# One decoder step on one core: v and a of an RWKV-7 chunk transposed together from a side-by-side copy, and the two rank-64 products written in turns

## Chip, core and metric

One core of a Trainium2 chip runs the whole step. The metric is the device time of one execution in microseconds (us); less is better. TensorE is called PE, its weight loads PEld, VectorE DVE, ScalarE ACT, GpSimd POOL; SP is the SyncE queue that issues most DMAs.

## What is computed

The step is one layer over 1024 prompt tokens and 8 sequences of 8 sample tokens (1088 columns): an input projection into four token mixers (HGRN2, RWKV-7, a convolution module, RG-LRU), gates, output projection and an MLP, all in float32. The change touches the RWKV-7 mixer (8 heads of 64) and one scratch tile of the residual update. Cut from the reference:

```python
r, k, v, wd, ad, gd = split(rwm)                     # 512, 512, 512, 64, 64, 128 columns
log_w = -RW_DECAY_SCALE * sigmoid(rw_w0 + tanh(wd) @ rw_w_up)     # decay, rank 64
a = sigmoid(rw_a0 + ad @ rw_a_up)                                  # rate, rank 64
...
def step(s, inp):                                    # per token; s is [value, key] of a head
    rt, wt, kt, vt, kkt, at = inp
    sa = einsum("bhvk,bhk->bhv", s, -kkt)
    s = s * wt[:, :, None, :] + sa[..., None] * (kkt * at)[:, :, None, :] + vt[..., None] * kt[:, :, None, :]
    return s, einsum("bhvk,bhk->bhv", s, rt)
```

## The kernel before

Activations lie with channels on the 128 partitions and tokens along the row. Large products run as float32 split into two fp32r halves (tiles `pg`, weights `whi` and `wlo`, made from a staged load `wst` by ACT and DVE; `wst` has three buffers, `whi` and `wlo` four). Small products (`sm`, `tr`, `G`, `p1`, `wt`, `pu` and so on) are plain float32, for which the hardware makes two passes over PE; a transpose by `nc.tensor.transpose` takes one.

The mixers are Python generators. `ROUNDS` says in which order their pieces are written; a scheduler that simulates a timeline then interleaves the instructions of all of them on each engine, and the order on every engine is fixed from then on. PE so works on chunk products of the projections and gates (`pg`) while the chains of the mixers run on the other engines.

`rw_block(j)` handles two heads, 128 partitions, and runs four times (j = 0 to 3). In order:

- Two rank-64 products, decay and rate. `up[:, 0, :]` holds the decay matrix on partitions 0 to 63 and the rate matrix on 64 to 127, `wd` the two inputs in the same way. `small_mm` runs the rate product over three token tiles (364, 362 and 362 columns), each copied out of PSUM by ACT with a sigmoid, and then the decay product. PSUM tiles of the pool `pm` (tag `m`) have three buffers.
- From these, scaled forms per chunk of 64 tokens: `ar[chunk]` with the columns a (index 0, minus kk times decay; this is the "a" of the change, not the rate) and r (index 1), and `kb` with k and b. Products `G` per chunk and head, each on 64 of the 128 rows, alternate the heads, four chunks (8 products) to a group with two PSUM tiles. A triangular inverse follows: `za`, `At`, 31 steps on DVE with the scratch `tm`, then `zx`, `X1`, and the products `zq` and `zz`.
- A loop over 17 chunks, first number 16 (the sample tokens), then 0 to 15. On every even chunk it handles two chunks at once: v and a are transposed into one PSUM tile `tr` so that v's tokens lie on partitions 0 to 63 and a's on 64 to 127, kb is transposed beside them, and ACT copies the result to `vk` (two buffers). The products `p1` and `wt` use it, two chunks at a time. Per chunk then `pu`, a copy by ACT into `vk` (`vk<-pu`), `pst`, the state `St` by DVE, and `pyr`; `pu` of the next chunk needs `St`. So 32 pairs of chunks and 4 single chunks are transposed in the four blocks.

`add_resid` adds a scaled PSUM tile to the residual; its scratch `t64` is written and read by DVE.

Of the kernel before, what the change touches and what calls it, by code (L numbers as in the profile page):

```python
# [9 lines left out]
F32 = mybir.dt.float32  # L10
# [3 lines left out]
AF = mybir.ActivationFunctionType  # L14
# [10 lines left out]
CHUNKS = ((0, 364), (364, 362), (726, 362))  # L25
# [57 lines left out]
def c3(a):  # L83
    return a.rearrange("p (c t) -> p c t", t=64)


def s3(a):
    return a.rearrange("p (s t) -> p s t", t=8)


class Net:
# [382 lines left out]
    def rw_block(self, j):  # L474
        nc = self.nc
        J = slice(j * 128, j * 128 + 128)
        blk = self.c("blk")
        up = self.rp.tile([128, 2, 128], F32, name="up", bufs=1)
# [9 lines left out]
        def parts(x):  # L488
# [6 lines left out]
        ar = pair("ar", 8)  # L495
        ch = lambda x, c: x[c // 8][:, c % 8]

        a, sg, wd = self.flat("a", 4), self.flat("sg", 5), self.flat("wd", 2)
        nc.sync.dma_start(wd[:, :NT], self.wdd)
        kk, inv = self.flat("kk", 6), self.flat("inv", 3)  # L500
        self.act(kk[:, :NT], kF[:, :NT], AF.Square, scale=self.p("rw_k_k", j))
        self.small_mm(up[64:128, 0, :], wd[64:128, :],
                      lambda ps, n0, n: self.act(a[:, n0:n0 + n], ps[:, :n], AF.Sigmoid, bias=self.p("rw_a0", j)))
        self.small_mm(up[0:64, 0, :], wd[0:64, :],
                      lambda ps, n0, n: self.act(sg[:, n0:n0 + n], ps[:, :n], AF.Sigmoid, bias=self.p("rw_w0", j)))
        self.log_table()

        self.small_mm(blk, kk, lambda ps, n0, n: nc.vector.tensor_scalar(
# [43 lines left out]
        for c in range(0, 17, 4):  # L552
            w = min(4, 17 - c)
            pss = [self.pmt("G") for _ in range(2)]
            for cc in range(w):
                for h in range(2):
                    H = slice(64 * h, 64 * h + 64)
                    o = cc * 128
# [13 lines left out]
        v = self.flat("v", 12)  # L572
# [10 lines left out]
        nc.sync.dma_start(At, za.rearrange("a u i t -> (a u) i t"))  # L583
        nc.gpsimd.memset(Zu_t[0:68, 0:1024], 0.0)
        nc.gpsimd.memset(Zu_t[0:68, 0:1024:33], 1.0)
        tm_t = self.rp.tile([128, 256], F32, name="tm")
        for i in range(31):
            r, m = i + 1, 31 - i
            tm = tm_t[0:68, 0:r * m].rearrange("p (r m) -> p r m", m=m)
# [11 lines left out]
        for g in range(5):  # L601
            u0, w = 8 * g, (8 if g < 4 else 2)
# [3 lines left out]
        for u0 in range(0, 34, 16):  # L606
            w = min(16, 34 - u0)
            ps = self.pmt("zq")
# [16 lines left out]
        ident = self.c("ident")  # L625
# [3 lines left out]
        for c in [16] + list(range(16)):  # L629
            G = Gc(c)  # L630
            if c % 2 == 0:
                w = min(2, 17 - c)
                vk2 = self.rp.tile([128, 2, 2, 128], F32, name="vk", bufs=2)
                ps = self.pmt("tr")
                for cc in range(w):
                    o = cc * 256
                    nc.tensor.transpose(ps[0:64, o:o + 128], v[:, (c + cc) * 64:(c + cc) * 64 + 64], ident)
                    self.mm(ps[64:128, o:o + 128], ch(ar, c + cc)[:, 0, :], ident)
                    nc.tensor.transpose(ps[:, o + 128:o + 256], ch(kb, c + cc).rearrange("p a t -> p (a t)"), ident)
                self.act(vk2[:, 0:w].rearrange("p c a t -> p (c a t)"), ps[:, :w * 256])  # L640
                p12 = self.rp.tile([128, 2, 128], F32, name="p12", bufs=2)
                wt2 = self.wz[(c // 2) % 2]
                ps, ps2 = self.pmt("p1"), self.pmt("wt")
                for cc in range(w):
                    for h, Hc in enumerate(Hs):
                        self.mm(ps[64:128, cc * 128 + 64 * h:cc * 128 + 64 * h + 64], Gc(c + cc)[0:64, h, 0:64],
                                vk2[0:64, cc, 0, Hc])
                        self.mm(ps2[Hc, cc * 64:cc * 64 + 64], vk2[64:128, cc, 0, Hc], Zc(c + cc, h))
                self.act(p12[64:128, 0:w].rearrange("p c t -> p (c t)"), ps[64:128, :w * 128])
                for h, Hc in enumerate(Hs):  # L650
                    self.act(wt2[Hc, 0:w, h, :], c3(ps2[Hc, 0:w * 64]))
            cc = c % 2
            VA, KBT = vk2[:, cc, 0, :], vk2[:, cc, 1, :]

            if c < 16:
                pu = self.pc.tile([128, 512], F32, name="pu", tag="pc")
                for h, Hc in enumerate(Hs):
                    self.mm(pu[64:128, Hc], Zc(c, h), p12[64:128, cc, Hc], start=h == 0, stop=c == 0)
                if c:
                    for h, Hc in enumerate(Hs):  # L660
                        self.mm(pu[64:128, Hc], wt2[:, cc, h, :], St, start=False, stop=True)
            else:
                pu, px = self.pmt("pus"), self.pmt("px")
                for q in range(8):
                    for h, Hc in enumerate(Hs):
                        self.mm(px[Hc, 8 * q:8 * q + 8], ss[Hc, q, :], wt2[Hc, cc, h, 8 * q:8 * q + 8])
                ut = self.rp.tile([128, 64], F32, name="ut")
                self.act(ut, px[:, :64])
                self.mm(pu[64:128, 0:128], ut, ident, start=True, stop=False)
                for h, Hc in enumerate(Hs):  # L670
                    self.mm(pu[64:128, Hc], Zc(c, h), p12[64:128, cc, Hc], start=False, stop=True)
            self.act(VA[64:128, :], pu[64:128, 0:128])

            So = St
            if c < 16:
                pst = self.pc.tile([128, 512], F32, name="pst", tag="pc")
                for Hc in Hs:
                    self.mm(pst[Hc, 0:64], KBT[:, Hc], VA[:, Hc])
                Sn = self.rp.tile([128, 64], F32, name="St", bufs=3)
                if c == 0:  # L680
                    nc.vector.tensor_scalar(Sn, pst[:, 0:64], dec[:, 0:1], None, op0=OP.mult)
                else:
                    sp = self.rp.tile([128, 64], F32, name="sp", bufs=2)
                    nc.gpsimd.tensor_scalar(sp, St, dec[:, c:c + 1], None, op0=OP.mult)
                    self.stt(Sn, pst[:, 0:64], dec[:, c:c + 1], sp, OP.mult, OP.add)
                St = Sn
                if c == 15:
                    nc.gpsimd.dma_start(self.A["o_rw"][j, :, 0, :], St)

            if c % 8 == 0:  # L690
                py = self.py.tile([128, 512], F32, name="pyr", tag="py")
            yc = slice((c % 8) * 64, (c % 8) * 64 + 64)
            for h, Hc in enumerate(Hs):
                self.mm(py[Hc, yc], VA[:, Hc], G[:, h, 64:128], start=c % 8 == 0, stop=False)
            if c == 16:
                for q in range(8):
                    for Hc in Hs:
                        self.mm(py[Hc, 8 * q:8 * q + 8], ss[Hc, q, :], ar[2][Hc, 0, 1, 8 * q:8 * q + 8],
                                start=False, stop=q == 7)
            elif c:  # L700
                for Hc in Hs:
                    self.mm(py[Hc, yc], So[Hc, :], ch(ar, c)[Hc, 1, :], start=False, stop=True)
            if c % 8 == 7:
                self.act(y[:, (c - 7) * 64:(c + 1) * 64], py)
            elif c == 16:
                self.act(y[:, T:NT], py[:, :64])
                vx_t = self.flat("vx", 1)
                pst = self.pmt("pss")
                for h, Hc in enumerate(Hs):
                    vx = vx_t[:, h * 512:h * 512 + 512].rearrange("p (q v) -> p q v", v=64)  # L710
                    self.tt(vx, VA[:, Hc].unsqueeze(1).to_broadcast([128, 8, 64]),
                            self.c("bm").unsqueeze(2).to_broadcast([128, 8, 64]), OP.mult)
                    self.mm(pst[Hc, :], KBT[:, Hc], vx_t[:, h * 512:h * 512 + 512])
                self.tt(ss, ss, pst.rearrange("p (q v) -> p q v", v=64), OP.add)
                self.tt(ss, ss, dec[:, 16:24].unsqueeze(2).to_broadcast([128, 8, 64]), OP.mult)
                nc.gpsimd.dma_start(self.A["o_rw"][j, :, 1:9, :], ss)
# [370 lines left out]
def trunk_kernel(ctx: ExitStack, tc: tile.TileContext, A):  # L1087
# [158 lines left out]
    def add_resid(r, n0, ps, n, mt, gi, fresh=False):  # L1246

        e = min(n, T - n0)
        rp, pp = (r, ps) if e == n else (r[:, :e], ps[:, :e])
        if fresh:  # L1250
            net.act(rp, pp, scale=net.modp(gi, mt))
        else:
            net.stt(rp, pp, net.modp(gi, mt), rp, OP.mult, OP.add)
        if e < n:
            t = s3(r[:, e:n]) if fresh else net.kp.tile([128, 8, 8], F32, name="t64", tag="t64", bufs=2)
            net.tt(t, ps[:, e:n].rearrange("p (s t) -> p s t", t=8), net.mods(gi, mt), OP.mult)
            if not fresh:
                net.tt(r[:, e:n], r[:, e:n], t.rearrange("p s t -> p (s t)"), OP.add)
# [288 lines left out]
```

## Time and profile before

| | |
|---|---|
| Median of 3 runs | 2547.24 us (2545.0 to 2548.16) |
| The profiled execution, its own time | 2543.26 us |
| Its span, first to last instruction | 2541.4 us |
| Mean granted TensorE clock | 0.986 of full speed |
| PE busy | 2454.6 us, 97% |
| DVE, ACT, POOL busy | 54%, 41%, 13% |

The profile shows one execution. Times in its rows are us from the span's start unless they say ns. A timeline row has start, length, engine, line, operation, tile written and tiles read, size and count; rows of one kind that follow each other are merged, so that a length is that of the group. PE's lengths overlap, because products are pipelined and their ends are modelled: what a product costs is read from its start to the start of what follows it. [...] In a row of waits the engine and tile before the arrow wait for what stands behind it.

### The profile page before, as it was taken

The numbers are of one execution on the slowest core, as the hardware profiler recorded it, in microseconds if no ns is written. First come the engines' busy times: TensorE is split into PE (matmuls) and PEld (weight loads), VectorE is DVE, ScalarE is ACT, GpSimd is POOL, SyncE is SP. The second block draws the span as 40 slices with busy tenths as digits, with TensorE's granted clock in tenths as the row PEclk, the third lists the DMA queues.
The fourth block names the chain that finished last, engine by engine and source line by source line (L and its number), as shares of the span: only waits on it lengthen the run. The fifth ranks groups of instructions, "written<-read, shape, count | busy, mean of one in ns | idle before, by whom it ended". The sixth has DMA issues, their size and how long they took to land.

```text
span 2541.4 us, 46737 instructions
## 1 busy us (share of the span) xinstructions
PE 2454.6 (97%) x19222; PEld 2259.4 (89%) x19222; DVE 1381.6 (54%) x2536; ACT 1038.2 (41%) x1855; POOL 320.4 (13%) x503
## 2 busy tenths in 40 slices
PE   6999999999999999999999999999999999999996
PEld 2897889897898988989887999998899999999996
DVE  6664626647355645266552757668755552422246
ACT  4512434422454224453234753336666664111114
POOL 3101110102100011101021100000222221000003
PEclk9999999999999999999999999999999999999998
DMA  6322132122221222212312555533556657434144
GB/s 241 119 81 80 50 107 68 61 69 80 100 68 65 73 82 66 95 62 77 92 48 71 186 168 187 205 112 103 156 154 162 157 152 256 136 135 186 62 158 129
DMA packets 166550, 296.01 MB, mean 116 GB/s; under 512 B 38824, under 2 KB 78712, under 8 KB 166336
## 3 DMA queue, kind: packets, MB, share of 16 engines
q1 hardware_dynamic: 115920, 213.33, 26.0%
q0 software_dynamic: 47104, 74.44, 9.6%
q10 hardware_dynamic: 3312, 5.25, 0.6%
q8 instruction: 151, 2.47, 0.4%
q14 instruction: 63, 0.52, 0.1%
HBM read 211.29 MB, written 81.66 MB: 115 GB/s over the span
## 4 chain that ended last, share of the span: by engine, by line
PE 82%; DVE 9%; DMA 4%; ACT 2%; issue 2%; SPq 0%; DVEq 0%; ACTq 0%
PE pg L107 54%; PE pa L107 5%; PE pe L107 4%; PE sm L107 3%; DVE X L101 2%; PE ada L107 2%; PE pc L107 2%; PE pu L107 2%; PE pb L107 2%; DMA zx<-At 1%; DVE wlo L101 1%; PE pyr L107 1%; PE G L107 1%; PE tr L107 1%; PE po L107 1%
## 5 line engine op out<-in xcount | busy, mean ns | idle before, releaser
L107 PE MATMUL pg<-Hh,whi 128*128 128x362 f32 (+1 forms) x1872 | 627.7, 335 | 4.7 <-ACT Hh L98 4.2
L107 PE MATMUL pg<-Hh,wlo 128*128 128x362 f32 (+1 forms) x1872 | 631.3, 337 | 0.0
L107 PE MATMUL pg<-Hl,whi 128*128 128x362 f32 (+1 forms) x1872 | 623.3, 336 | 0.7 <-DVE Hl L104 0.6
L98 ACT ACTIVATE whi<-wst 128x512 fp32r<-128x512 f32 (+1 forms) x404 | 249.8, 619 | 620.9 <-PE pg L107 546.5
L101 DVE TENSOR_TENSOR wlo<-wst,whi 128x512 fp32r<-128x512 f32 (+1 forms) x404 | 279.8, 694 | 389.1 <-ACT whi L98 384.6
L107 PEld LDWEIGHTS pg<-Hh,whi 128*128 128x128 f32 x1872 | 356.2, 190 | 15.4 <-ACT Hh L98 6.2
L107 PEld LDWEIGHTS pg<-Hh,wlo 128*128 128x128 f32 x1872 | 356.6, 190 | 13.8 <-issue 6.5
L107 PEld LDWEIGHTS pg<-Hl,whi 128*128 128x128 f32 x1872 | 355.3, 190 | 10.8 <-issue 2.5
L107 PE MATMUL pg<-ah,whi 128*128 128x272 f32 x960 | 276.3, 290 | 4.0 <-ACT whi L98 4.0
L107 PE MATMUL pg<-ah,wlo 128*128 128x272 f32 x960 | 277.2, 290 | 0.9 <-DVE wlo L101 0.9
L107 PE MATMUL pg<-al,whi 128*128 128x272 f32 x960 | 273.9, 290 | 0.0
L107 PEld LDWEIGHTS pg<-ah,whi 128*128 128x128 f32 x960 | 181.9, 190 | 4.9 <-ACT whi L98 4.7
L107 PEld LDWEIGHTS pg<-ah,wlo 128*128 128x128 f32 x960 | 182.1, 190 | 1.7 <-DVE wlo L101 1.5
L107 PEld LDWEIGHTS pg<-al,whi 128*128 128x128 f32 x960 | 180.4, 190 | 0.0
L104 DVE SCALAR_TENSOR_TENSOR cacc<-u,pv,cacc 128x1024 f32<-128x1024 f32 x120 | 154.3, 1286 | 2.1
L104 DVE SCALAR_TENSOR_TENSOR R<-pg,mod,R 128x544 f32<-128x544 f32 (+2 forms) x120 | 65.7, 570 | 134.7 <-PE pg L107 134.6
L107 PE MATMUL pg<-yh,whi 128*128 128x362 f32 (+1 forms) x384 | 127.6, 332 | 0.9 <-DVE gt L101 0.9
L107 PE MATMUL pg<-yh,wlo 128*128 128x362 f32 (+1 forms) x384 | 126.6, 330 | 0.0
L107 PE MATMUL pg<-yl,whi 128*128 128x362 f32 (+1 forms) x384 | 126.2, 329 | 0.0
L1172 POOL DMA_DIRECT2D g<-gst x96 | 53.5, 558 | 400.5 <-ACT gst L98 396.8
L98 ACT ACTIVATE gst<-pg 128x362 f32<-128x362 f32 (+1 forms) x96 | 45.5, 474 | 132.4 <-PE pg L107 112.3
L104 DVE SCALAR_TENSOR_TENSOR St<-pst,dec,sp 128x64 f32<-128x64 f32 x60 | 17.0, 283 | 136.4 <-PE pst L107 135.3
(450 smaller groups left out, 4884.0 us busy)
## 6 DMA issues: line engine op xcount, KB each, us to landing
wst<-w SPq DMA_DIRECT2D x136, 256.0 KB, 2.9
wst<-w_in SPq DMA_DIRECT2D x92, 256.0 KB, 3.0
gt<-g SPq DMA_DIRECT2D x32, 544.0 KB, 3.8
wst<-w_gate SPq DMA_DIRECT2D x64, 256.0 KB, 3.5
adaw<-ada SPq DMA_DIRECT2D x32, 512.0 KB, 3.9
ah<-ah POOLq DMA_DIRECT2D x60, 272.0 KB, 2.8
al<-al POOLq DMA_DIRECT2D x60, 272.0 KB, 4.3
ah<-ah SPq DMA_DIRECT2D x30, 544.0 KB, 9.7
```

The lines of the kernel that those rows point to most:

```text
L98: return self.nc.scalar.activation(out, in_, func, bias=bias, scale=scale)
L101: return self.nc.vector.tensor_tensor(out, a, b, op=op)
L104: return self.nc.vector.scalar_tensor_tensor(out, a, s, b, op0=op0, op1=op1)
L107: return self.nc.tensor.matmul(out, lhsT, rhs, start=start, stop=stop, skip_group_check=True)
L1172: nc.gpsimd.dma_start(d[:, n0:n0 + n], t[:, :n])
```

## The change

- The copy: two DMAs per pair of chunks bring v and a side by side into `va` (three buffers), on the SP queue. One full transpose per chunk takes the place of a transpose of v and a product of a with the identity, each of which filled half of the columns of PE.
- The rank-64 products: per token tile first the rate, then the decay product, and then their two sigmoids; they take turns where all three of the one stood before all three of the other.
- Room: the scratch `tm` shares the two buffers of `vk`, and `t64` has one buffer.

```diff
-        self.small_mm(up[64:128, 0, :], wd[64:128, :],
-                      lambda ps, n0, n: self.act(a[:, n0:n0 + n], ps[:, :n], AF.Sigmoid, bias=self.p("rw_a0", j)))
-        self.small_mm(up[0:64, 0, :], wd[0:64, :],
-                      lambda ps, n0, n: self.act(sg[:, n0:n0 + n], ps[:, :n], AF.Sigmoid, bias=self.p("rw_w0", j)))
+        for n0, n in CHUNKS:
+            pa, pw = self.pmt("sm"), self.pmt("sm")
+            for ps, H in ((pa, slice(64, 128)), (pw, slice(0, 64))):
+                self.mm(ps[:, :n], up[H, 0, :], wd[H, n0:n0 + n])
+            self.act(a[:, n0:n0 + n], pa[:, :n], AF.Sigmoid, bias=self.p("rw_a0", j))
+            self.act(sg[:, n0:n0 + n], pw[:, :n], AF.Sigmoid, bias=self.p("rw_w0", j))
...
-        tm_t = self.rp.tile([128, 256], F32, name="tm")
+        tm_t = self.rp.tile([128, 512], F32, name="tm", tag="vk", bufs=2)
...
-                vk2 = self.rp.tile([128, 2, 2, 128], F32, name="vk", bufs=2)
+
+                va = self.rp.tile([128, 2, 2, 64], F32, name="va", bufs=3)
+                nc.sync.dma_start(va[:, 0:w, 0, :], c3(v[:, c * 64:(c + w) * 64]))
+                nc.sync.dma_start(va[:, 0:w, 1, :], ar[c // 8][:, c % 8:c % 8 + w, 0, :])
+                vk2 = self.rp.tile([128, 2, 2, 128], F32, name="vk", tag="vk", bufs=2)
                 ps = self.pmt("tr")
                 for cc in range(w):
                     o = cc * 256
-                    nc.tensor.transpose(ps[0:64, o:o + 128], v[:, (c + cc) * 64:(c + cc) * 64 + 64], ident)
-                    self.mm(ps[64:128, o:o + 128], ch(ar, c + cc)[:, 0, :], ident)
+                    nc.tensor.transpose(ps[:, o:o + 128], va[:, cc].rearrange("p a t -> p (a t)"), ident)
                     nc.tensor.transpose(ps[:, o + 128:o + 256], ch(kb, c + cc).rearrange("p a t -> p (a t)"), ident)
...
-            t = s3(r[:, e:n]) if fresh else net.kp.tile([128, 8, 8], F32, name="t64", tag="t64", bufs=2)
+            t = s3(r[:, e:n]) if fresh else net.kp.tile([128, 8, 8], F32, name="t64", tag="t64", bufs=1)
```

Where the instructions stand now. On PE, in the first block, the rank-64 products (`sm<-wd,up`, one row per product, the count behind it; `ada` is a product for the modulation that the scheduler put between them). A minus is before, a plus is now:

```order
-L107 MATMUL sm<-wd,up 128x364
-L107 MATMUL sm<-wd,up 128x362 x2
+L107 MATMUL sm<-wd,up 128x364 x2
+L107 MATMUL sm<-wd,up 128x362
 L107 MATMUL ada<-adaw,cs 32x512 x8
-L107 MATMUL sm<-wd,up 128x364
-L107 MATMUL sm<-wd,up 128x362 x2
+L107 MATMUL sm<-wd,up 128x362 x3
 L107 MATMUL ada_1147<-cv,adaw 128x16 x4
```

Before, three rate products stood ahead of `ada` and three decay products behind it. Now rate, decay, rate stand ahead and decay, rate, decay behind. In the other three blocks the six stood as two, one and three with `ada` between; that split has stayed, now as a rate and a decay product, one rate product, and then decay, rate, decay.

On PE, at the single chunk 16 of the first block, the transposes (`cv` holds the identity, `ars` and `kbs` are the sample chunk's forms, the `zz` product belongs to the inverse):

```order
 L107 MATMUL zz<-Gs,X_1530 32x32 x2
-L637 MATMUL tr<-cv,v 64x128
-L107 MATMUL tr<-cv,ars 64x128
-L639 MATMUL tr<-cv,kbs 128x128
+L643 MATMUL tr<-cv,va 128x128
+L644 MATMUL tr<-cv,kbs 128x128
 L107 MATMUL pg<-Hh_117,whi 128x362
```

Two instructions over half of the columns have become one over all of them. A pair of chunks has the same twice, and nearly everything around the transposes stays in its place; in most pairs 13 `pg` products now stand between the transposes and the next `pst` where 11 stood.

On the SP queue, in the first block behind the loads of the inverse, among the loads of weights (`wst`) and of the modulation matrix (`adaw`). Before:

```order
L159 DMA wst<-w_in 128x512 x4
L350 DMA adaw<-ada 128x1024 x3
L159 DMA wst<-w_gate 128x512
L350 DMA adaw<-ada 128x1024
```

Now, at the same place:

```order
L159 DMA wst<-w_in 128x512 x2
L637 DMA va<-v 128x2x64
L638 DMA va<-ar_986 128x2x64
L159 DMA wst<-w_in 128x512 x2
L350 DMA adaw<-ada 128x1024 x3
L159 DMA wst<-w_gate 128x512
L637 DMA va<-v 128x2x64
L638 DMA va<-ar_986 128x2x64
L350 DMA adaw<-ada 128x1024
```

The copies of chunks 4 and 5 and of chunks 6 and 7 have come between loads that PE needs in time. Those of chunk 16 and of chunks 0 to 3 stand further ahead, before the loads of the inverse.

## Rows read from the trace of the kernel before

**Rows 1.** The page: busy time of each engine (share of the span), instructions.
```profile
PE 2454.6 (97%) x19222; PEld 2259.4 (89%) x19222; DVE 1381.6 (54%) x2536; ACT 1038.2 (41%) x1855; POOL 320.4 (13%) x503
```

**Rows 2.** Windows: stretch, length, busy time by engine, clock, DMA, GB/s.
```profile
70.00:500.00 430.00, 424.19 (x3331) 377.73 (x3329) 234.61 (x459) 171.06 (x324) 54.17 (x97) 0.99 0.26 81
...
1000.00:1500.00 500.00, 493.04 (x4197) 435.18 (x4196) 262.47 (x448) 225.46 (x376) 57.06 (x107) 1.00 0.28 92
```

**Rows 3.** Timeline of PE in the first block: start us, us, instruction.
```profile
270.78 0.30 PE L637 MATMUL tr<-cv,v 128*64 128x128 f32 x1
...
271.37 0.33 PE L639 MATMUL tr<-cv,kb 128*128 128x128 f32 x1
...
272.19 0.41 PE L107 MATMUL pg<-Hl,whi 128*128 128x362 f32 x1
...
274.19 0.34 PE L107 MATMUL pst<-vk 128*64 128x64 f32 x4
...
289.11 0.30 PE L637 MATMUL tr<-cv,v 128*64 128x128 f32 x1
```

**Rows 4.** Timeline of PE in the HGRN2 block: eight full-width transposes in a row.
```profile
419.11 0.27 PE L862 MATMUL htr<-cv,hV 128*128 128x128 f32 x1
...
419.88 0.27 PE L863 MATMUL htr<-cv,kd 128*128 128x128 f32 x1
419.90 0.41 PE L107 MATMUL pg<-Hl,whi 128*128 128x364 f32 x1
```

**Rows 5.** Timeline of PE in the second block: the rank-64 products (sm<-wd,up).
```profile
448.76 1.48 PE L107 MATMUL sm<-wd,up 64*128 64x364 f32 x4
450.17 1.04 PE L107 MATMUL ada<-adaw,cs 128*32 128x512 f32 x2
451.15 0.87 PE L107 MATMUL sm<-wd,up 64*128 64x362 f32 x2
451.95 1.92 PE L107 MATMUL ada<-adaw,cs 128*32 128x512 f32 x14
453.80 2.09 PE L107 MATMUL sm<-wd,up 64*128 64x364 f32 x6
455.82 0.84 PE L107 MATMUL ada<-cv,adaw 128*128 128x16 f32 x6
```

**Rows 6.** Windows of the G products alone: stretch, length, PE busy (instructions).
```profile
132.60:133.00 0.40, 0.40 (x12) 1.00 0.00 0
133.40:133.80 0.40, 0.40 (x6) 1.00 0.00 0
```

**Rows 7.** Instructions on tile G: ns min/median/max, first and last start.
```profile
L107 PE MATMUL G<-ar,kb x256: 272/272/373, 132.2 to 1177.9; 64*128 64x128 f32 x128
```

**Rows 8.** Waits of PE, 70 to 1500 us: total, times, longest.
```profile
PE zq L107 <- DMA X<-zx: 13.3, 4, 3.4
...
PE pst L107 <- ACT vk L98: 1.1, 3, 0.4
```

**Rows 9.** Timeline of ACT just ahead of the transposes at 270.78.
```profile
270.28 0.27 ACT L98 ACTIVATE vk<-pu 64x128 f32<-64x128 f32 x1 [3.08 <-PE pu L107]
```

**Rows 10.** DMA issues: queue, count, KB each, median us to landing.
```profile
za<-G SPq DMA_DIRECT2D x32, 32.0 KB, 2.1
G<-zb SPq DMA_DIRECT2D x32, 32.0 KB, 2.5
```

**Rows 11.** Waits of the SP queue over the span: total, times, longest.
```profile
SPq L159 <- DVE wlo L101: 1012.3, 195, 23.9
```

**Rows 12.** Waits of ACT, 70 to 1500 us.
```profile
ACT whi L98 <- PE pg L107: 237.3, 69, 8.9
```

**Rows 13.** Instructions on tile sm: the copy of a rate tile out of PSUM.
```profile
L98 ACT ACTIVATE a<-sm,pv x12: 555/562/573, 106.1 to 1140.7; 128x362 f32<-128x362 f32 x8, 128x364 f32<-128x364 f32 x4
```

**Rows 14.** Timeline of DVE ahead of the G products of the first block.
```profile
128.87 0.22 DVE L101 TENSOR_TENSOR kbs<-kF,sg 128x64 f32<-128x64 f32 x1
```

**Rows 15.** Timeline of PE: the first G products of the first block.
```profile
132.22 2.05 PE L107 MATMUL G<-ar,kb 64*128 64x128 f32 x24
```

## Prediction

> **What bounds the kernel now.** I read the page's busy times first: PE is busy for 97% of the span and the next engine, DVE, for 54% [rows 1]. [...] The largest is 13.3 us in four waits, one per block, for the inverse's DMA; it begins with the last G product, behind the rank-64 products and ahead of the transposes, and its length hangs on neither. At the chunk loop itself PE waited only 1.1 us, three times, for ACT's copy ahead of `pst` [rows 8]. So the work on PE sets the time of this stretch: what a product takes less there comes off, as long as nothing else becomes late. The sum is therefore a sum of PE time, read from start to start, since the lengths overlap.
>
> **The transposes.** A pair of chunks takes v, a in two passes and kb, twice, on PE. The reader is to see in [rows 3] the first transpose at 270.78 and the next chunk product at 272.19: 1.41 us. The first kb starts at 271.37, so v and a of one chunk take 0.59. The runs before other successors are some 0.1 to 0.2 longer; I keep the shorter one. What replaces them is not in that loop, but the HGRN2 block has it: eight transposes over all 128 columns, starting from 419.11 to 419.88, are 0.11 apart, and the product behind the last starts 0.02 later [rows 4]. Four such are 3 x 0.11 + 0.02 = 0.35 us. The row in HGRN2 follows products over the full array; here 64x64 products stand ahead. How much longer the first takes for that no row shows; I bound it by 0 and by 0.11, one transpose, and take 0.05. So a pair gains 1.41 - 0.35 - 0.05 = 1.01 us, bounds 0.95 and 1.06, and 32 pairs gain 32.3 us (30.4 to 33.9). Four single chunks I estimate at half a pair, 0.5 each: 2.0. Together 34.3 us. ACT's copy out of `tr` keeps its size.
>
> **The rank-64 products.** Each fills 64 of the 128 rows of PE. In the second block two tiles in a row take 1.41 us (448.76 to 450.17), one 0.80 (451.15 to 451.95), three 2.02 (453.80 to 455.82) [rows 5]: 4.23 us for six, 0.61 for each further tile of a run. Whether two products on the two halves of the rows run at once, the G products tell. A pass lasts 0.272 us [rows 7], so a window of 0.40 us touches the passes that started within 0.672 us. In a window at 132.60, where products of both heads alternate, there are 12, one per 0.056 us; at 133.40, where only one head's are left since the third PSUM buffer belongs to it, 6, one per 0.112 [rows 6]. Alternating halves run two at a time. In the new order a rate and a decay tile then take 0.80, the lone rate tile 0.80, and decay, rate, decay as two in series 1.41: 3.01 us, 1.22 less. The first block has two runs of three, 2 x 2.02, and gets two of 1.41: also 1.22. Four blocks gain 4.9 us. It is not lost at the next dependent products: G starts at 132.22 [rows 15], and the last of its operands was ready at 128.87 + 0.22 = 129.09 [rows 14], 3.1 us ahead.
>
> The bound below is nothing. The three PSUM buffers are emptied by ACT at 0.562 us a tile [rows 13], six tiles 3.4 us, more than the 3.01 that PE now needs; if PE then stands waiting for a buffer, the gain goes. I take the upper end, since `ada` products of about 1 and 1.9 us stand between the runs [rows 5] and give ACT that time. [...]
>
> **What the shorter transposes uncover.** They also hid the chain of a chunk: `pu`, ACT's copy, `pst`, the state on DVE, the next `pu`. In the loop's body the copy ends at 270.28 + 0.27 = 270.55 [rows 9] and `pst` starts at 274.19 [rows 3]: 3.64 us in hand, of which 1.06 go and 0.33 come back with the two `pg` products that the scheduler moved in. There it costs nothing. The first three or four pairs of a block run closely together with only an `ada` product between; the waits of up to 0.4 us stand there [rows 8]. I price new waits at 0.5 us a block, 2.0 in all (0 to 4 there).
>
> **The copies.** 72 DMAs are added, two for each of 36 runs of transposes, of 32 KB or 64 KB. The nearest rows are the 32 KB moves of the inverse on the same queue: 2.1 and 2.5 us from issue to landing [rows 10]. They cost nothing if they land early. `va` has three buffers, so a copy can be issued when the transposes three runs earlier are done; two runs of the body are 289.11 - 270.78 = 18.3 us apart [rows 3], and the close first ones have their copies issued ahead of the inverse or behind chunk 16. Without that cover each run would stand for 2.1 to 2.5 us. Queued behind a copy that waits for its buffer are loads of weights and of `adaw`. But SP already stood at weight loads 195 times for 1012.3 us in all, 5.2 us each, since a staging buffer was not free [rows 11], and in this stretch ACT's split of weights waited for PE, 69 times for 237.3 us, with the weights landed [rows 12]. A load that is a few us late meets that slack.
>
> **The rest.** `tm` takes a buffer that the second last `vk` of the block before has long left, and both instructions on `t64` run on DVE, in order; neither costs anything, as the DVE at 54% would hide even a small wait.
>
> **The sum.** 34.3 + 4.9 - 2.0 = 37.2 us off the profiled execution's 2543.26 (2541.4 of it the span): 2506.1. The median of the runs shown is 2547.24, 4.0 above that execution, so I predict 2510 for a median.
>
> **Rivals.**
>
> *The chain takes half of it back.* If ACT and DVE answer later than the 3.6 us in hand suggest, because their own work is placed differently, each pair waits some 0.5 us: 16 us, and the median is 2526. For it speaks that PE waits for ACT's copy already; against it that the waits are 1.1 us in 1430.
>
> *The turns bring nothing*, the change's second half not doing what it says: ACT empties PSUM too slowly, or the halves do not overlap at 362 columns as at 128. Then 2515. [Rows 6] speak against the second.
>
> *The copies come late: slower.* If a run's copy is issued only just ahead of its transposes, because SP stands at something else, PE waits 2.5 us at each of 32 pairs, 80 us, against 37 gained: 2590. From 37.2 / 32 = 1.16 us of waiting a pair on, the change is a loss. The 18.3 us between runs and the place of the copies in the queue speak against it; for it, that one late item holds back the whole queue.
>
> **Chances and range.** As forecast 0.70, with a range of its own of 2504 to 2517 (the bounds of the terms, 33 to 41 us, and the spread of 2 us that the runs show). Half taken back 0.18. No gain from the turns 0.06. Copies late 0.06, of which 0.04 so far that the kernel is slower by more than 0.2% and 0.02 near no change. No change is what lies within 0.2% of before, about what a measurement of this kernel can tell; 0.2% is 5 us. That makes faster 0.94, the same 0.02, slower 0.04. The range reaches to the first rival: 2503 to 2528.
>
> **What would show it.** In the profile after: runs of four `tr` products 0.11 apart, some 0.4 us in all; `sm<-wd,up` in pairs, 0.80 for the first two tiles; PE's waits in the stretch with `zq` still near 3.3 us a block. Wrong it would be if `tr` waits for DMA `va`, if `pst`, `p` or `pu` wait for ACT for more than 0.1 us a chunk, if `pg` waits for `whi`, or if the end comes earlier in the loop but PE stands longer at `zq` or at the HGRN2 levels.

## Result, and the profile after

The changed kernel takes 2526.16 us (median of 4 runs, 2519.98 to 2534.61) against 2547.32 for the kernel before on the same chip: a ratio of 0.9917, 95% interval 0.9898 to 0.9936. It was run a second time:

> The changed kernel once more, as the one to compare with on this chip: 2526 (2520 to 2535), with stops of 2 to 3 us inside the lv products of blocks two to four and PE's waits for the scratch t of add_resid (2.8 and 0.7 us) in the output projection, if these belong to the program. If they were an accident of the one execution profiled, they are gone or stand elsewhere.

2526.28 us (5 runs, 2524.74 to 2528.32), ratio 0.9910, 0.9896 to 0.9923. The stops and the waits came again, at the same instructions (2.99, 2.14 and 1.48 us inside `lv`; the first of the two in the output projection is put down to another engine, with the same 2.76 us).

So 21 us came off where 37 were forecast: the direction and the range 2503 to 2528 held, the value of 2510 and its own range of 2504 to 2517 did not. The profiled execution took 2528.64 us, 2526.9 of it the span.

The page, busy times, as in [rows 1]:

```profile
PE 2430.2 (96%) x19086; PEld 2255.0 (89%) x19086; DVE 1381.1 (55%) x2536; ACT 1037.1 (41%) x1855; POOL 330.2 (13%) x503
```

PE lost 24.4 us of busy time and 136 products in the trace: per chunk, one pass for v and two for a became one, 68 times. Timeline of PE at the pair that answers to [rows 3]:

```profile
265.98 0.33 PE L643 MATMUL tr<-cv,va 128*128 128x128 f32 x1
266.14 0.27 PE L644 MATMUL tr<-cv,kb 128*128 128x128 f32 x1
266.25 0.27 PE L643 MATMUL tr<-cv,va 128*128 128x128 f32 x1
266.36 0.27 PE L644 MATMUL tr<-cv,kb 128*128 128x128 f32 x1
266.38 0.41 PE L107 MATMUL pg<-Hh,whi 128*128 128x364 f32 x1
```

From the first transpose to the next chunk product 0.40 us, where it was 1.41. The rank-64 products of the second block, as [rows 5], same view:

```profile
443.23 0.88 PE L107 MATMUL sm<-wd,up 64*128 64x364 f32 x4
444.04 1.06 PE L107 MATMUL ada<-adaw,cs 128*32 128x512 f32 x6
445.03 0.87 PE L107 MATMUL sm<-wd,up 64*128 64x362 f32 x2
445.83 1.90 PE L107 MATMUL ada<-adaw,cs 128*32 128x512 f32 x10
447.66 1.48 PE L107 MATMUL sm<-wd,up 64*128 64x362 f32 x6
449.08 0.73 PE L107 MATMUL ada<-cv,adaw 128*128 128x16 f32 x5
```

The six tiles take 0.81, 0.80 and 1.42, 3.03 us in all, against 4.23. Both parts of the change do on PE what was forecast. The waits of PE, 70 to 1500 us, tell where time went (compare [rows 8]):

```profile
PE zq L107 <- DMA X<-zx: 13.2, 4, 3.5
PE lv L107 <- issue: 9.2, 5, 3.0
PE ada L107 <- DMA adaw<-ada: 2.1, 4, 0.9
PE lv L107 <- DVE X L101: 1.9, 3, 0.8
PE pst L107 <- ACT vk L98: 1.1, 3, 0.4
```

`zq` and `pst` are as before; no transpose waits for a copy. New are the second and the third row. Inside the `lv` products of HGRN2's levels PE stands 9.2 us and waits for nothing that the profile names. And products for the modulation (`ada`) wait for their matrix, once in each block among the first transposes. That belongs to the transposes' part of the change, since a kernel with the turns alone (below) has no such wait. The longest ended at 244.09 us with the landing of a load that SP had issued at 236.80 between copies of v and a; it took 7.25 us, where 5.7 was the longest before that the profile tells of. The page's DMA issues, before and now:

```profile
adaw<-ada SPq DMA_DIRECT2D x32, 512.0 KB, 3.9
```

```profile
adaw<-ada SPq DMA_DIRECT2D x32, 512.0 KB, 5.3
```

So the change has a cost of some 2 us here, at a load beside the copies. That the copies ahead of it in the queue make it late is likely but not shown: PE also needs the matrix sooner. And in the output projection, 1640 to 1760 us, there is a row that the kernel before did not have:

```profile
PE pg L107 <- DVE t L101: 3.5, 2, 2.8
```

The stages, read from the start of their first row on PE to the start of their last, one profile each (us; blocks one to four):

| | loop over chunks, `tr` to `tr` | levels, `lv` to `htr` | output projection |
|---|---|---|---|
| before | 102.8, 102.8, 102.9, 114.3 | 35.9, 35.9, 35.9, 41.5 | 98.1 |
| changed | 97.5, 95.4, 95.0, 105.2 | 36.1, 40.9, 39.1, 46.2 | 101.6 |
| changed, second profile | 95.6, 95.6, 95.0, 105.1 | 36.1, 38.3, 38.9, 44.1 | 101.6 |
| 32 products at the head (below) | 95.6, 95.7, 95.3, 105.1 | 37.1, 36.0, 36.0, 41.5 | 102.2 |
| the same, t64 with two buffers | 95.7, 95.8, 94.9, 105.1 | 37.1, 36.0, 36.0, 41.5 | 98.1 |

The loops gave 29.7 and 31.5 us. The levels took back 13.1 and 8.1 and the output projection 3.5.

### The profile page after: what moved, and what is told of

It reads as the page before. It is cut to its first block, busy times and chain, and to the rows that moved or that the text cites. A ratio compares the mean times of both kernels' runs of the same rounds, so it can differ in the third digit from the quotient of the medians.

```text
span 2526.9 us, 46611 instructions
## 1 busy us (share of the span) xinstructions
PE 2430.2 (96%) x19086; PEld 2255.0 (89%) x19086; DVE 1381.1 (55%) x2536; ACT 1037.1 (41%) x1855; POOL 330.2 (13%) x503
## 4 chain that ended last, share of the span: by engine, by line
PE 79%; DVE 9%; DMA 6%; issue 3%; ACT 3%; SPq 0%; DVEq 0%; ACTq 0%; POOL 0%; POOLq 0%
PE pg L107 52%; PE pa L107 6%; PE pe L107 4%; PE sm L107 2%; PE pc L107 2%; PE pb L107 2%; PE ada L107 2%; PE pu L107 2%; DMA zx<-At 1%; DVE X L101 1%; DVE wlo L101 1%; PE G L107 1%; DMA adaw<-ada 1%; PE pyr L107 1%; PE po L107 1%
## 5 line engine op out<-in xcount | busy, mean ns | idle before, releaser
L689 POOL TENSOR_SCALAR sp<-St,dec 128x64 f32<-128x64 f32 x60 | 56.1, 935 | 231.0 <-DVE St L104 209.1
```

## What stands in the levels

`lv` is a run of 100 products of 32x32 for three levels: 200 passes on PE, 400 rows of the trace with the weight loads, in about 2 us. All engines' rows in the second block of the changed kernel, timeline (idle time before a row in brackets):

```profile
742.28 1.73 PE L107 MATMUL lv<-X 128*32 128x32 f32 x167
742.49 0.71 DVE L101 TENSOR_TENSOR X<-X,hq 128x544 f32<-128x544 f32 x1
743.23 1.29 DVE L101 TENSOR_TENSOR hq<-hq,eb 128x1088 f32<-128x1088 f32 x1
...
747.02 0.66 PE L107 MATMUL lv<-X 128*32 128x32 f32 x33 [3.02 <-issue]
```

The last operand, `X`, was written by 743.20; PE stops at 744.01 in the middle of the run, and the product at 747.02 carries no wait for a semaphore, so neither an operand nor a PSUM buffer is late. The page's DMA queues name another traffic:

```profile
q8 instruction: 150, 2.46, 0.4%
```

That is 150 packets of 16 KB, for 38,441 rows of PE in the trace (products, weight loads, semaphores): one packet per 256 rows. The kernel before has 151 packets and 38,675 rows. I read them as PE's instructions, which arrive in blocks of 256. In the window 744.0 to 744.7 us no such packet moves, in the next, 744.7 to 745.8, there is one:

```profile
q8 instruction: 1, 0.02, 5.3%
```

The packet has landed at 745.70, and PE goes on 1.32 us later, at 747.02. It is so each time: the traces of these experiments have 32 stops marked "issue" of 0.4 us or more in the `lv` products, in eleven profiles, and PE goes on 1.3 to 1.5 us after such a packet has landed, always 193 or 194 rows behind a multiple of 256. And the stops keep a step of their own: counted in PE's rows they begin at number 11457, 17089 and 22722, which is 5632 and 5633 apart, 22 x 256, while the program's blocks repeat after 5578 rows. Theory: the `lv` run uses up 256 instructions in 1.3 us, faster than the next block comes; if the ends of two blocks fall into one run or just behind it, PE runs dry. How long a stop lasts the theory does not give: in the first block of the changed kernel two ends fall into the run as well, and PE stood only 0.5 us, since the packet had landed 0.7 us before PE stopped; what decides when a packet sets out no row shows. The change took some 58 rows out of each block and so moved these ends; in the kernel before, by the same count, one lay in each run, some 220 rows in (170 in the fourth block), and the next behind it. The rival is the place that the scheduler gave the work on DVE (`X`, `hq`, `hacc`), which also changed there.

## Experiments

Ratios are to the kernel before on the same chip, with the 95% interval.

**The two ends of the theory.** Products on constants at the head of PE's program, where PE waits for its first data, move the ends of the blocks and nothing else: the order on every engine is otherwise that of the kernel without them.

```diff
+            pad = pct("pad")
+            for _ in range(32):
+                net.mm(pad[0:32, 0:32], net.ones[:, 0:32], net.ones[:, 0:32])
```

> The changed kernel with 32 products of 32x32 on constants put at the head of PE's program, where PE waits for its first data; nothing else changes its place on any engine. They add 128 rows of PE to the trace (two passes, each with its weight load). Theory 'PE's instruction blocks': the ends of the blocks move by half a block against the lv products; the stop inside them goes from 3.0 to below 0.5 us in the second block and from 2.4 to below 0.6 in the third, the one in the fourth (2.3) falls to below 1, and the first block gets one of about 2.5 at the end of its run instead of 0.5. Together some 5 us less standing and fewer stretches at half clock behind it: 2515 to 2521 against 2526. Rival 'the order on DVE or the PSUM buffers bring the stops': the orders are the same, so the stops stay where they are, and the time is 2526.

2515.65 us (4 runs, 2513.83 to 2519.27), ratio 0.9874, 0.9861 to 0.9887; in a second comparison (front_after_again) 2516.96, ratio 0.9887, 0.9873 to 0.9902. PE's timeline in the second block of the first of the two:

```profile
743.54 2.17 PE L107 MATMUL lv<-X 128*32 128x32 f32 x200
746.51 0.33 PE L867 MATMUL htr<-cv,hV 128*128 128x128 f32 x1 [0.80 <-DVE hacc L791]
```

The 200 passes run through. Of the waits "issue" 0.8 us is left in the stretch, in the third block (1.3 us in the repeat), where below 0.6 had been expected. The first block's levels took 1.0 us more than in the changed kernel, where a stop of 2.5 had been expected at the end of the run. 32 idle products make the kernel some 10 us faster.

> The changed kernel with 32 products at the head of PE's program, once more, to have it on one chip with the two that follow: 2515.7 (2513 to 2520), with the HGRN2 levels as quick as before the change in blocks two to four.

The same in the kernel before, 36 products:

> The kernel before with 36 products of 32x32 on constants at the head of PE's program, nothing else changed. Theory 'PE's instruction blocks': the ends of the blocks move by 144 rows, so that in the first three blocks one falls some 80 rows into the run of 200 lv passes and the next inside it: stops of 2.3 to 3 us come in three blocks, 0.5 or less in the fourth, with stretches at half clock behind them. 7 to 13 us more: 2554 to 2560 against 2547.3. Rival 'the stops belong to the changed order of the instructions': none comes, and the time stays within 1 us of before.

2551.7 us (11 runs) against 2548.14, ratio 1.0022, 1.0011 to 1.0033: slower, but by 3 to 8 us where 7 to 13 had been expected. PE's waits, 70 to 1500 us, and its timeline in the second block:

```profile
PE lv L107 <- issue: 6.2, 3, 2.3
...
755.50 1.72 PE L107 MATMUL lv<-X 128*32 128x32 f32 x167
759.46 0.46 PE L107 MATMUL lv<-X 128*32 128x32 f32 x33 [2.24 <-issue]
```

It stops after the same 167 passes, 1.7, 2.2 and 2.3 us in three blocks. Counted in PE's rows these stops begin at 6082, 11713 and 17345, each 256 behind a stop of the changed kernel (5826, 11457 and 17089): the same place in a block, in a program that differs ahead of it. The levels there take 37.0, 37.4, 40.6 and 41.5 us, 7.2 more than before: in the first two blocks a stop costs less than its length, since PE had waited there in any case, and only behind the third did the clock fall, to 0.75 over the 6.8 us that follow.

With 64 products, 256 rows, a whole block:

> The kernel before with 64 products of 32x32 at the head: 256 rows of PE, a whole block of its instructions, so each block ends at the same products as before. Theory 'PE's instruction blocks': no new stop inside the lv products and a time within 1.5 us of before. Rival 'the products at the head cost time themselves or delay the start': up to 3 us more, as much again as 36 products did or more, and visible ahead of 60 us in the trace.

2547.88 us (11 runs), ratio 0.9996, 0.9986 to 1.0006, no "issue" wait at `lv`. So the products themselves cost nothing that shows in the median (in the one profile the first block's rank-64 products begin 4.4 us later than before, at 109.4 us); what counts is the number of rows modulo 256. The theory stands, and the rival falls, since in the traces the order of all 2536 instructions on DVE is the same in each pair.

**The clock behind a stop.** Windows of the changed kernel around the stop: stretch, its length, busy times of PE, PEld, DVE, ACT and POOL, and behind them the granted clock as a share of its full speed, the share of the DMA engines and GB/s:

```profile
742.00:744.00 2.00, 2.00 (x170) 1.71 (x169) 1.97 (x3) 0.00 (x0) 0.00 (x0) 1.00 0.38 115
744.00:747.00 3.00, 0.01 (x2) 0.00 (x0) 1.39 (x4) 0.00 (x0) 0.00 (x0) 0.84 0.05 16
747.00:753.80 6.80, 6.78 (x59) 6.71 (x59) 1.21 (x3) 1.82 (x3) 2.31 (x7) 0.57 0.02 4
753.80:760.00 6.20, 6.20 (x50) 6.20 (x50) 2.37 (x6) 2.83 (x8) 0.00 (x0) 1.00 0.13 42
```

and the one that answers to the third of them with 32 products at the head:

```profile
745.60:752.00 6.40, 5.54 (x49) 5.22 (x39) 2.88 (x8) 2.46 (x5) 2.33 (x7) 1.00 0.07 22
```

After the 3 us of standing PE ran 6.8 us at a mean granted clock of 0.57, with 0.50 from 748 to 752 us; without the stop it stayed at 1.00. Eight `htr` transposes then start 0.21 apart instead of 0.11. So this stop cost more than its length. The second execution of the same kernel had the same stop there (2.99 us), the clock stayed at 1.00, and the levels took 38.3 us instead of 40.9.

**The two parts alone.** The turns in the kernel before, and the transposes without the turns, with the stops and without them:

```diff
-        self.small_mm(up[64:128, 0, :], wd[64:128, :], ...)
-        self.small_mm(up[0:64, 0, :], wd[0:64, :], ...)
+        for n0, n in CHUNKS:
+            pa, pw = self.pmt("sm"), self.pmt("sm")
...
```

> The kernel before with only the rank-64 products in turns. Theory 'the terms add': 1.22 us less in each of four blocks, 4.9 us in all, so about 2542.4 against 2547.3; the number of PE's instructions stays, so PE's rows in the HGRN2 levels (lv) keep their waits of before (1.35 us and 0.4 to 0.7 us, none above 2 us). Rival 'taken back at the next wait': PE stands longer at zq by as much, and the time stays at 2547.

2542.93 us (11 runs), ratio 0.9975, 0.9966 to 0.9984: 5.2 us less, and `zq` waits 13.2 us as before. The rival falls.

> The changed kernel with the rank-64 products in the order of before. If the terms add, it is 4.9 us above the changed kernel, 2531 against 2526. The theory 'PE's instruction blocks' (PE runs dry inside the quick lv products because the end of a block of 256 instructions falls there) expects the same stops inside the lv products as in the changed kernel, 2 to 3 us in blocks two to four, since the count of PE's instructions is the same. The rival 'the products in turns moved the work behind them and brought the stops' expects no stops above 1.4 us and about 2520.

2526.92 us (4 runs), ratio 0.9914, 0.9901 to 0.9928, with stops of 2.85, 2.19 and 1.45 us at the very rows 11457, 17089 and 22722. That answers the question of the stops; the 4.9 us of the turns don't show between 0.9914 and the changed kernel's 0.9917 and 0.9910, whose intervals are wider than 4.9 us. With the stops out of the way:

> The kernel above (32 products at the head, t64 with one buffer) with the rank-64 products in the order of before; eight rows of PE a block pair change place, nothing else. With the stops inside the lv products out of the way, the turns should show their 4.9 us: 2520.6 against 2515.7. If the turns bring nothing once the transposes are quick, 2515.7.

2522.74 us (6 runs, 2517.11 to 2527.23), ratio 0.9908 against 0.9887 for the kernel with the turns on the same chip: 5.8 us by the medians, though the two intervals overlap. Together with the first of the three, whose interval is 4 to 9 us, the term of 4.9 is borne out. The transposes alone, without the stops, bring 23 us (20 to 27 by the interval).

**The scratch t64.** What one buffer does is seen in DVE's timeline, at one tile of the output projection (the first of the two instructions that empty its PSUM tile starts 71.4 us behind the projection's start in both kernels). They are `rh<-pg,mod,rh` and `t<-pg,mod`. Before:

```profile
1730.90 0.22 DVE L101 TENSOR_TENSOR rh<-rh,t 128x64 f32<-128x64 f32 x1
...
1734.90 0.43 DVE L104 SCALAR_TENSOR_TENSOR rh<-pg,mod,rh 128x208 f32<-128x208 f32 x1
1735.25 0.22 DVE L101 TENSOR_TENSOR t<-pg,mod 128x64 f32<-128x64 f32 x1
```

and in the changed kernel, with PE's next row:

```profile
1717.39 0.22 DVE L101 TENSOR_TENSOR rh<-rh,t 128x64 f32<-128x64 f32 x1
...
1717.88 0.43 DVE L104 SCALAR_TENSOR_TENSOR rh<-pg,mod,rh 128x208 f32<-128x208 f32 x1
...
1722.91 0.22 DVE L101 TENSOR_TENSOR t<-pg,mod 128x64 f32<-128x64 f32 x1
```

```profile
1723.14 0.36 PE L107 MATMUL pg<-Mh,whi 128*128 128x272 f32 x1 [2.76 <-DVE t L101]
```

The two stood 0.35 us apart and now stand 5.03 apart, and PE goes on as the second ends. The reader of the `t` before (`rh<-rh,t`) had ended at 1717.61. So what held the write back was its late place in DVE's order, which the scheduler has to put somewhere behind that reader; why as late as this no row shows.

The experiment gives it two buffers, from the projection's own pool:

```diff
-net.kp.tile([128, 8, 8], F32, name="t64", tag="t64", bufs=1)
+(scratch or net.kp).tile([128, 8, 8], F32, name="t64", tag="t64", bufs=2 if scratch else 1)
...
-                    add_resid(r, half * HALF + n0, ps[:, :n], n, mt, 2)
+                    add_resid(r, half * HALF + n0, ps[:, :n], n, mt, 2, scratch=ops[half])
```

> The changed kernel with two buffers for the scratch t64 in the output projection, in another pool that has room there. Theory 'one buffer holds PSUM back': DVE's write of t, which empties a PSUM tile, has to stand behind the reader of the t before, and PE waited for it for 2.8 and 0.7 us; with two buffers both waits go, and the time is 3.5 us under the changed kernel. Rival 'the stage after it takes the time back' (the MLP's first products wait for DVE and ACT in any case): the waits go and the time is within 1 us of the changed kernel.

2518.46 us (5 runs, 2513.19 to 2527.42), ratio 0.9879, 0.9861 to 0.9897, against 0.9910 on the same chip: 7.8 us by the medians, but with a spread of 14. The scheduler also made another order with it, on DVE from the projection on and on PE behind it, so this is not a test of the buffer alone. With the products at the head as well:

> The changed kernel with the 32 products at the head of PE's program and with two buffers for t64. If the two losses are separate they add: 10 us for the stops and 3.5 for t, 2512 against 2526, which is near the 2510 that the prediction gave. If they are one loss seen twice, about 2516.

2516.19 us (4 runs), ratio 0.9872, 0.9858 to 0.9885, where one buffer had 0.9874: nothing. Once more, both on one chip:

> The same with two buffers for t64, once more, since the first comparison left open whether the time follows the stage. In the profiles the output projection takes 98.1 us with two buffers and 101.6 to 102.2 with one. If that reaches the end, 3.5 us under the kernel above, 2512; if the MLP behind it waits for the same DVE and ACT work in any case, within 1 us of it.

2514.53 us (4 runs, 2512.86 to 2515.75), ratio 0.9875, 0.9862 to 0.9888, against 2516.96 and 0.9887: 2.4 us. The one wait of PE that is left in its output projection (1625 to 1740 us) is that of before:

```profile
PE pg L107 <- ACT Mh L98: 1.3, 1, 1.3
```

So the wait for `t` is gone and the projection takes 98.1 us as before, in all three profiles. What of these 3.5 us reaches the end stays open: the three comparisons give 7.8, about 0 and 2.4. In the profiles the rest of PE's program, from the projection's last row to PE's last, took 769 to 774 us with one buffer (six profiles) and 771 to 776 with two (three). That speaks for some of it being taken back there, but the profiles with one buffer differ by as much among themselves.

**The copies.** One buffer for `va`:

```diff
-                va = self.rp.tile([128, 2, 2, 64], F32, name="va", bufs=3)
+                va = self.rp.tile([128, 2, 2, 64], F32, name="va", bufs=1)
```

> The changed kernel with one buffer for va in place of three, so that a copy is issued only when the transposes of the run before are done. The prediction held that the copies cost nothing as they land early. In the body of the loop the runs are 14 to 19 us apart, and 2.0 us of landing is still hidden; the second and third pair of a block follow the one before by 2.2 to 2.4 us, less than issue and landing of two copies: PE should stand some 1 to 3 us at each, 10 to 25 us in all: 2536 to 2551. If the copies are hidden there too (the scheduler moves other products ahead), within 3 us of the changed kernel, 2526.

2530.8 us (5 runs, 2521.46 to 2531.9), ratio 0.9939, 0.9926 to 0.9952: 4.5 us by the medians and 7 by the ratios more than with three buffers, not 10 to 25. PE's waits, 70 to 1500 us:

```profile
PE tr L643 <- DMA va<-ar: 1.6, 4, 0.8
```

Waits at the transposes come, but short ones; the order had also been made anew around them. What the other 3 to 5 us are stays open: the profiled execution was the quickest of the five. The copies are far from the 1.16 us a pair at which the change would be a loss.

## Why the prediction was right in part

- **PE bounds the stretch.** Right in the main; the stretch is the 70 to 1500 us of [rows 8], and PE was busy for 98.6% of each of the two parts of it in [rows 2]. The turns, tried alone, came off the end in full. The transposes, tried without the stops, took 31.2 us off the loops, but 26 off the end of the profiled execution and 23 off the median: the levels (1.2) and the output projection (3.8) took back 5, and the rest lies within the difference of single executions.
- **Transposes, 34.3 less 2.0 for new waits.** Right: the loops fell by 7.3, 7.2, 7.9 and 9.2 us in the second profile, 31.5 in all, against 32.3. That the term of 2.0 for new waits fits is luck: it was meant for the chain of a chunk, and `pst` waits 1.1 us as before; what came is the 2.1 us of `ada`.
- **Turns, 4.9.** Right, 5.2 and 5.8 measured. The bound of nothing, by which PE stands for ACT's copies out of PSUM, did not come: the tiles take 3.03 us on PE against 3.01 forecast, with `ada` products between the runs.
- **Copies, nothing.** Right for the transposes, which wait for no copy with three buffers. Wrong for "A load that is a few us late meets that slack": the loads of `adaw` came late, and PE waited 2.1 us for them.
- **`t64`, "neither costs anything, as the DVE at 54% would hide even a small wait".** This step failed. It looked at DVE's own waits. But DVE's write of `t` is the last to empty a PSUM tile, and with one buffer it got a place 5.0 us behind the other instead of 0.35; PE waited 2.8 and 0.7 us for it.
- **The sum, "read from start to start", with nothing for the places that PE's rows move past.** This is the step that cost most: some 10 us (2526 to 2516 with 32 idle products). The instruction stream was shorter by some 58 rows a block, and two ends of its blocks of 256 then fell inside the quick `lv` runs.

The sum with these two terms is 37.2 - 10 - 3.5 = 23.7 us if the 3.5 count in full, which stays open, and 21 were measured, with an interval of 16 to 26. The last sign that the prediction named for being wrong, PE standing longer at the HGRN2 levels, is the one that came. The first rival has the time, 2526, but not the mechanism: the chain of a chunk took nothing back. So it is luck that the time lies in the range of 2503 to 2528: its upper end was drawn for a loss that did not come, and losses that the sum had at nothing came in its place.

The quickest kernel here is the changed one with 32 products at the head and two buffers for `t64`, ratio 0.9872 and 0.9875, 32 us under the kernel before; the second buffer's share of that is not settled.

## What to carry to other kernels

A sum of time on PE is not complete without the count of its instructions: where some hundred tiny products follow each other, see in which of PE's rows a stop marked "issue" begins, and whether these numbers are a multiple of 256 apart. A few idle products where PE waited anyway moved the stops here, and are a cheap control for any change that adds or removes instructions ahead of such a run. And a scratch tile used by one engine alone is not private to it if its writer also empties a PSUM tile: with one buffer that writer got a later place in the order here.

## What was not expected of the hardware

- What I read as PE's instructions came in packets of 16 KB, one per 256 rows (150 packets for 38,441 rows), and did not come in time: PE stood up to 3.1 us inside runs of products 0.01 us apart. The packet's move took about 0.9 us (5.3% of 16 engines in 1.1 us), and PE went on 1.3 to 1.5 us after it had landed; what fills this last time no row shows.
- Two executions of the changed kernel's levels differ by 4.9 us, with stops in the same rows. In the second block the stops are equally long, and the granted clock fell to a mean of 0.57 behind the one and stayed at 1.00 behind the other: 2.6 of the 4.9 us. What decided that no row shows.
